# Every weight tile as three 256-column products, with one displacement between weights and moving tiles in SBUF

## The chip, the core and the metric

The kernel runs on one core of a Trainium2 chip. The metric is the device time of one execution in microseconds. The kernel before takes 1125.85 us, the median of three runs (1125.81 to 1126.93).

## What is computed

A trunk of two layers (DEPTH = 2) works on 256 positions of 1024 channels in float32. Each layer is a gated feed-forward block, a mixer, and a second feed-forward block, each behind an RMS norm and added to the residual; a last RMS norm ends it.

```python
for l in range(DEPTH):
    x = x + 0.5 * swiglu_ffn(rmsnorm(x, norm_ffn1[l]), ffn1_w_up[l], ffn1_w_down[l])
    x = x + hybrid_mixer(rmsnorm(x, norm_mix[l]), w_in[l], pool_w[l], pool_b[l], ...)
    x = x + 0.5 * swiglu_ffn(rmsnorm(x, norm_ffn2[l]), ffn2_w_up[l], ffn2_w_down[l])
return rmsnorm(x, final_norm)
...
def swiglu_ffn(h, w_up, w_down):
    a, b = jnp.split(h @ w_up, 2, axis=-1)
    return (jax.nn.silu(a) * b) @ w_down
```

The up weights are 1024 x 5632, the down weights 2816 x 1024. The mixer projects 1024 channels to 5120 (a pooling branch of 4 groups, a recurrent branch of 10 heads, a GELU branch, gate logits), sends the two branches through projections of their own, and ends with a 1024 x 1024 output projection (w_out).

## The kernel before, in words

**Weight tiles.** All weights come from DRAM as one stream of 128 x 128 tiles in the order in which they are used, 3152 of them, 8 to a transfer (`raw`). Each float32 value is split in two fp32r parts: ACT writes the high part (`wh`, a Copy at L219), DVE the low one (`wl`, a subtraction at L228). The moving tiles are split in the same way: high and low part of the 256 positions lie beside each other. A product of weights and activations is the sum wh·xh + wh·xl + wl·xh.

**Two forms of a tile.** `mm` (L309 to L320) makes three matmuls of 256 columns into one half of a PSUM bank (L316: wh·xh, L317: wh·xl, L318: wl·xh). `mm_wide` (L322 to L332) makes two: wl·xh, 256 columns, into the bank's first half (L329), and wh over both parts of x, 512 columns, into the whole bank (L330). After it the bank's second half holds wh·xl, which has to be added to the first.

```python
t.matmul(ps.t[:, 0, :], lhsT=wl(), rhs=x()[:, 0, :], start=start, stop=False, skip_group_check=True)
t.matmul(ps.t, lhsT=wh(), rhs=x(), start=False, stop=stop, skip_group_check=True)
```

**Which stage uses which.** The feed-forward blocks (`ffn`, L414) and the mixer's output projection (`out_mm`, L711) use the wide form; the rest of the mixer uses `mm`, and so does the very last output tile. Of the 3152 tiles 2218 are wide: four up products of 352 tiles with the moving tile XS, four down products of 176 (the last one 154) with GA and GB, two output projections of 64 with MU and MI. The other 934 are narrow: XS 640, ZHL 160, PHL 72, VHL 40, GA and GB 22.

**Evacuation.** In `evac` (L424) each up result of the wide form takes an ACT copy of the bank's second half and a DVE addition, twice per hidden tile, then one DVE multiplication with the norm's factor `rt` over 512 columns, SiLU on ACT, the gate's product on DVE and the split. In `new_x` (L393) the wide form takes an ACT copy into `sd` and a DVE addition beside the residual's update. Narrow pairs are evacuated by `scaled` (L384): one DVE multiplication of 512 columns straight from the bank, whose two halves hold two results.

**Order.** A planner (`Plan.schedule`, L123) orders DVE and ACT by due times that it reckons from costs, T_MM and T_MM_WIDE among them (L193, L194); PE and the transfers keep the program's order. The planner's costs are not measured by the program.

**Places in SBUF.** Pools are laid out one behind the other: the single tiles (XS among them), `raw`, `wh`/`wl`, a filler tile named `shift` (L846), then the large tiles by tag in the order in which they are first asked for. The tiles' sizes are multiples of 512 bytes except U, which has 10360 bytes. The built program has these first bytes of a partition:

| tile | first byte | modulo 512 | weights' place minus the tile's, modulo 512 |
|---|---|---|---|
| wh, wl (all 16) | 68864 and on | 256 | |
| XS | 24736 | 160 | +96 |
| VHL, ZHL, GA; GB | 134432; 156960 | 288 | -32 |
| MU | 189728 | 288 | -32 |
| PHL; MI | 210336; 218528 | 416 | -160 |
| acc; ones (the norm's moving tile and its weights) | 44736; 42112 | 192; 128 | -64 between these two |

A weight tile is 512 bytes of a partition, so within a chunk every tile has the same place modulo 512, and so has every moving tile of one name.

Of the kernel before, what the change touches and what calls it, by code (L numbers as in the profile page):

```python
# [8 lines left out]
F32 = mybir.dt.float32  # L9
F32R = mybir.dt.float32r  # L10
AF = mybir.ActivationFunctionType
ALU = mybir.AluOpType

D = 1024
S = 256
DEPTH = 2
KD = D // 128
FF = 2816
KF = FF // 128
# [4 lines left out]
NH = 10  # L24
CW = 4
# [11 lines left out]
HEAD = [[2, 2, 4], [4, 4], [4, 4], [4, 4]]  # L37
NRAW = 5
NSPL = 8
WARM = 7  # L40


# [147 lines left out]
    return 0.068 + 0.001042 * n + 0.06 * ptrs  # L190


T_MM = 0.327  # L193
T_MM_WIDE = 0.3245  # L194
KH = KF // 2


class Trunk:
# [120 lines left out]

        self.plan.add("PE", T_MM, fn, keys + list(r), [(ps, half)])  # L320

    def mm_wide(self, tag, ps, x, r, start, stop):  # L322

        wh, wl, keys = self.next_tile(tag)

        def fn():
            t = self.env.nc.tensor

            t.matmul(ps.t[:, 0, :], lhsT=wl(), rhs=x()[:, 0, :], start=start, stop=False, skip_group_check=True)  # L329
            t.matmul(ps.t, lhsT=wh(), rhs=x(), start=False, stop=stop, skip_group_check=True)  # L330

        self.plan.add("PE", T_MM_WIDE, fn, keys + list(r), [(ps, 0), (ps, 1)])  # L332


    def prep_x(self, m, gain, key):

# [41 lines left out]
    def x(self, m):  # L378
        return self.X.t[:, KD + m * S:KD + (m + 1) * S]
# [10 lines left out]
        self.mm(tag, ps, half, lambda: self.XS.t[:, k, 0, :], lambda: self.XS.t[:, k, 1, :],  # L390
                [(self.XS, (k, 0)), (self.XS, (k, 1))], k == 0, k == KD - 1)

    def new_x(self, m, ps, scale, gain, wide):  # L393
        X = self.X
        if wide:
            L = self.sd
            low = lambda: L.t
            self.act(low, lambda: ps.t[:, 1, :], AF.Copy, [(ps, 1)], [(L, 0)], S, scale=scale)
        self.stt(lambda: self.x(m), lambda: ps.t[:, 0, :], scale, lambda: self.x(m), ALU.mult, ALU.add,
                 [(ps, 0), (X, m)], [(X, m)], S)  # L400
        if wide:
            self.tt(lambda: self.x(m), lambda: self.x(m), low, ALU.add, [(X, m), (L, 0)], [(X, m)], S)
        if gain is not None:
            self.prep_x(m, self.par(gain + m), (self.prm, 0))
        self.prep_sq(m, gain is not None or m < KD - 1)
        if gain is None:
            if m == 0:
                self.XF = self.big("U", "XF", [128, KD, S], F32)
            XF = self.XF
            self.act(lambda: XF.t[:, m, :], lambda: self.x(m), AF.Copy, [(X, m), (self.prm, 0)], [(XF, m)], S,  # L410
                     scale=self.par(P_FIN + m))


    def ffn(self, l, wu, wd, gain, first):  # L414
        halves = (self.big("A", "GA", [128, KH, 2, S], F32R), self.big("B", "GB", [128, KH, 2, S], F32R))
        FT = self.big("V", "FT", [128, NH, S], F32)
        final = gain is None
        last = []

        def g(j):  # L420
            b = halves[j // KH]
            return b, (lambda: b.t[:, j % KH, :, :]), (b, (j, 0)), (b, (j, 1))

        def evac(j, ps):  # L424
            a, c = 2 * (j % 3), 6 + j % 3
            for h in range(2):
                t = lambda h=h: FT.t[:, a + h, :]
                self.act(t, lambda h=h: ps[h].t[:, 1, :], AF.Copy, [(ps[h], 1)], [(FT, a + h)], S)
                self.tt(t, lambda h=h: ps[h].t[:, 0, :], t, ALU.add, [(ps[h], 0), (FT, a + h)], [(FT, a + h)], S)
            both = lambda: FT.t[:, a:a + 2, :]  # L430
            tk = [(FT, a), (FT, a + 1)]
            self.tt(both, both, lambda: self.rt.t[:, None, :].to_broadcast([128, 2, S]), ALU.mult, tk + [(self.rt, 0)], tk,
                    2 * S)
            s = lambda: FT.t[:, c, :]
            last.append(self.act(s, lambda: FT.t[:, a, :], AF.Silu, [(FT, a)], [(FT, c)], S))
            self.tt(s, s, lambda: FT.t[:, a + 1, :], ALU.mult, [(FT, a + 1), (FT, c)], [(FT, c)], S)
            _, v, hi, lo = g(j)
            self.split(lambda: v()[:, 0, :], lambda: v()[:, 1, :], s, [(FT, c)], [hi], [lo], S)

        def up(ps, h, j, k):  # L440
            self.mm_wide((wu, l, k, h * KF + j), ps, lambda: self.XS.t[:, k, :, :],
                         [(self.XS, (k, 0)), (self.XS, (k, 1))], k == 0, k == KD - 1)

        ps = {}
        for h in range(2):
            for j in range(2):
                ps[j, h] = self.psum()
            for k in range(KD):
                for j in range(2):
                    up(ps[j, h], h, j, k)  # L450
                if h == (1 if first else 0) and k == (7 if first else 5):
                    self.norm_r(AF.Silu)
        for j in range(KF):
            if j >= 2:
                for h in range(2):
                    ps[j, h] = self.psum()
                    for k in range(KD):
                        up(ps[j, h], h, j, k)
            evac(j, (ps[j, 0], ps[j, 1]))
        self.preload(AF.Sqrt, last)  # L460
        for m in range(KD):
            pm = self.psum()
            wide = not (final and m == KD - 1)
            for k in range(KF):
                _, v, hi, lo = g(k)
                tag = (wd, l, k, m)
                if wide:
                    self.mm_wide(tag, pm, v, [hi, lo], k == 0, k == KF - 1)
                else:
                    self.mm(tag, pm, 0, lambda v=v: v()[:, 0, :], lambda v=v: v()[:, 1, :], [hi, lo], k == 0, k == KF - 1)  # L470
            self.new_x(m, pm, 0.5, gain, wide)


    def mixer(self, l, gain):
# [8 lines left out]
        g_at = 0  # L483
        u_at = KD * S
        s_at = u_at + PG * UW
        U = self.big("U", "U", [128, NH, CW - 1 + S], F32)
        V = self.big("V", "V", [128, NH, S], F32)
        TT = self.big("T", "TT", [128, NH, S], F32)
        PHL = self.big("P", "PHL", [128, 2 * PG, S], F32R)

        def G(m, n=1):
            return lambda: MB.t[:, g_at + m * S:g_at + (m + n) * S].rearrange("p (m t) -> p m t", t=S)
# [22 lines left out]
        ps = [self.psum(), self.psum()]  # L515
# [8 lines left out]
        for g in range(PG):  # L524
            sh = 1 << g
            lo = 2 * sh - 1
# [79 lines left out]


        R = self.big("U", "R", [128, NH, S], F32)
        I = self.big("I", "I", [128, NH, S], F32)

        def lru_gates(hs):
            for h in hs:
# [97 lines left out]

        def out_mm(ps, m, k):  # L711
            v, hi, lo = ms(k)
            self.mm_wide(("w_out", l, k, m), ps, v, [hi, lo], k == 0, k == KD - 1)

        ps = [self.psum(), self.psum()]
        for k in range(KD):
# [2 lines left out]
        for m in range(KD):  # L719
            if m >= 2:  # L720
                ps.append(self.psum())
                for k in range(KD):
                    out_mm(ps[m], m, k)
            self.new_x(m, ps[m], 1.0, gain, True)


    def softplus(self):
# [35 lines left out]
    def build(self):  # L763
# [1 line left out]
        self.head = [("L", 0), ("G", 0), ("L", 1), ("G", 1), ("L", 2), ("G", 2), ("L", 3), ("M", 0), ("L", 4), ("G", 3)]  # L765
        self.total = DEPTH * (2 * (2 * KF * KD + KD * KF) + 40 * KD + PG + 2 * NH + KD * PG + KD * NH + KD * KD)
        self.X = self.one("XG", [128, KD + KD * S])
        self.XS = self.one("XS", [128, KD, 2, S], F32R)
        self.prm = self.one("prm", [128, P_COLS])
        self.ones = self.one("ones", [128, 128])  # L770
        self.eps = self.one("eps", [128, 1])
# [66 lines left out]
def tile_trunk(ctx: ExitStack, tc: tile.TileContext, xt: bass.AP, par: bass.AP, wts: bass.AP, out: bass.AP):  # L838
# [4 lines left out]
    env.rawp = ctx.enter_context(tc.tile_pool(name="rawp", bufs=NRAW))  # L843
    env.splp = ctx.enter_context(tc.tile_pool(name="splp", bufs=NSPL))

    ctx.enter_context(tc.tile_pool(name="shift", bufs=1)).tile([128, 8], F32, name="shift")  # L846
    env.big = ctx.enter_context(tc.tile_pool(name="big", bufs=1))
    env.psp = ctx.enter_context(tc.tile_pool(name="psp", bufs=8, space=bass.MemoryType.PSUM))
    trunk.env = env
# [55 lines left out]
```

## Time and profile before

| | us |
|---|---|
| median of three runs | 1125.85 |
| the profiled execution | 1125.13 |
| its span, first to last instruction | 1123.4 |
| PE busy in it | 1109.6 (99%) |
| DVE busy | 885.2 (79%) |
| ACT busy | 691.1 (62%) |
| mean granted TensorE clock, share of full speed | 0.997 |

PE is the matmul stream, PEld the loading of weights into the array, which runs beside it. A matmul's record is longer than the distance to the next one's start, since matmuls are pipelined; the rate of the stream is read from starts, not from durations.

### The profile page before, as it was taken

How to read it: one execution, taken by the hardware profiler on the slowest of the kernel's cores; microseconds unless marked ns; L12 is line 12 of the kernel's file. 1: busy time of each engine (PE TensorE's matmuls, PEld its weight loads, DVE VectorE, ACT ScalarE, POOL GpSimd, SP SyncE). 2: the span in 40 equal slices, each digit the busy share in tenths (PEclk: the TensorE clock that was granted, in tenths of full speed). 3: DMA queues.
4: the chain of work that ended last, by engine and by line, in shares of the span. 5: the costliest groups of instructions: out<-in, count | busy, mean ns of one | idle time of the engine just before them, and what ended most of it. 6: DMA issues, size and time to landing. Idle time of an engine off the chain costs nothing.

```text
span 1123.4 us, 18938 instructions
## 1 busy us (share of the span) xinstructions
PE 1109.6 (99%) x7268; PEld 1016.8 (91%) x7268; DVE 885.2 (79%) x1384; ACT 691.1 (62%) x1133; POOL 0.2 (0%) x4
## 2 busy tenths in 40 slices
PE   8999999999999999999999999999999999999996
PEld 7888889999999888888888888899999998888886
DVE  7998766898988987776687777669989788777752
ACT  8766655559765765565565556555686666555641
POOL 0000000000000000000000000000000000000000
PEclk9999999999999999999999999999999999999998
DMA  8856666556656566666666666665476566666631
GB/s 287 271 180 205 188 188 189 185 170 191 193 182 188 188 191 191 192 192 189 188 188 188 189 189 192 195 182 185 142 229 184 173 205 187 189 188 189 188 111 38
DMA packets 59130, 210.03 MB, mean 187 GB/s; under 512 B 6560, under 2 KB 7456, under 8 KB 59040
## 3 DMA queue, kind: packets, MB, share of 16 engines
q1 hardware_dynamic: 59040, 208.82, 60.5%
q8 instruction: 57, 0.93, 0.3%
q14 instruction: 33, 0.27, 0.1%
HBM read 207.75 MB, written 1.05 MB: 186 GB/s over the span
## 4 chain that ended last, share of the span: by engine, by line
PE 98%; DMA 1%; DVE 0%; SPq 0%; ACT 0%; issue 0%; DVEq 0%; ACTq 0%
PE ps L330 45%; PE ps L329 23%; PE ps L316 10%; PE ps L317 10%; PE ps L318 10%; DMA XG<-in_x 1%; PE ps L360 0%; DVE XF L228 0%; DVE rt L370 0%; SPq L277 0%; SPq L791 0%; ACT XS L219 0%; PE ps L366 0%; DVE wl L228 0%; DVEq L900 0%
## 5 line engine op out<-in xcount | busy, mean ns | idle before, releaser
L219 ACT ACTIVATE wh<-raw 128x1024 fp32r<-128x1024 f32 (+2 forms) x399 | 418.3, 1050 | 365.3 <-PE ps L330 269.2
L228 DVE TENSOR_TENSOR wl<-raw,wh 128x1024 fp32r<-128x1024 f32 (+2 forms) x399 | 481.9, 1210 | 184.3 <-ACT wh L219 181.2
L330 PE MATMUL ps<-XS,wh 128*128 128x512 f32 x1408 | 488.7, 392 | 0.0
L329 PE MATMUL ps<-XS,wl 128*128 128x256 f32 x1408 | 394.7, 280 | 3.8 <-DVE wl L228 3.8
L330 PEld LDWEIGHTS ps<-XS,wh 128*128 128x128 f32 x1408 | 264.3, 188 | 58.2
L329 PEld LDWEIGHTS ps<-XS,wl 128*128 128x128 f32 x1408 | 264.3, 188 | 5.2 <-DVE wl L228 5.0
L316 PE MATMUL ps<-XS,wh 128*128 128x256 f32 x640 | 180.6, 282 | 0.0
L318 PE MATMUL ps<-XS,wl 128*128 128x256 f32 x640 | 180.2, 282 | 0.0
L317 PE MATMUL ps<-XS,wh 128*128 128x256 f32 x640 | 180.2, 282 | 0.0
L317 PEld LDWEIGHTS ps<-XS,wh 128*128 128x128 f32 x640 | 121.4, 190 | 0.1
L316 PEld LDWEIGHTS ps<-XS,wh 128*128 128x128 f32 x640 | 121.4, 190 | 0.1
L318 PEld LDWEIGHTS ps<-XS,wl 128*128 128x128 f32 x640 | 121.4, 190 | 0.0
L330 PE MATMUL ps<-GA,wh 128*128 128x512 f32 x341 | 119.6, 390 | 0.0
L330 PE MATMUL ps<-GB,wh 128*128 128x512 f32 x341 | 119.6, 390 | 0.0
L329 PE MATMUL ps<-GB,wl 128*128 128x256 f32 x341 | 96.2, 282 | 0.0
L329 PE MATMUL ps<-GA,wl 128*128 128x256 f32 x341 | 96.2, 282 | 0.0
L330 PEld LDWEIGHTS ps<-GA,wh 128*128 128x128 f32 x341 | 64.0, 188 | 13.4
L330 PEld LDWEIGHTS ps<-GB,wh 128*128 128x128 f32 x341 | 64.0, 188 | 13.4
L228 DVE TENSOR_TENSOR FT<-ps,FT 128x256 f32<-128x256 f32 x176 | 72.9, 416 | 1.8 <-ACT FT L219 1.7
L219 ACT ACTIVATE FT<-ps 128x256 f32<-128x256 f32 x176 | 64.3, 368 | 4.5 <-PE ps L330 4.1
L329 PEld LDWEIGHTS ps<-GB,wl 128*128 128x128 f32 x341 | 64.4, 189 | 0.0
L329 PEld LDWEIGHTS ps<-GA,wl 128*128 128x128 f32 x341 | 64.4, 189 | 0.0
(127 smaller groups left out, 1226.3 us busy)
## 6 DMA issues: line engine op xcount, KB each, us to landing
raw<-in_w SPq DMA_DIRECT2D x390, 512.0 KB, 4.2
raw<-in_w SPq DMA_DIRECT2D x7, 256.0 KB, 6.2
XG<-in_x SPq DMA_DIRECT2D x3, 256.0 KB, 6.0
out<-XF SPq DMA_DIRECT2D x3, 256.0 KB, 2.3
raw<-in_w SPq DMA_DIRECT2D x2, 128.0 KB, 3.1
out<-XF SPq DMA_DIRECT2D x2, 128.0 KB, 2.1
XG<-in_x SPq DMA_DIRECT2D x1, 132.0 KB, 2.6
XG<-in_x SPq DMA_DIRECT2D x1, 128.0 KB, 3.2
```

Source lines behind the costliest of these rows:

```text
L219: self.env.nc.scalar.activation(out=out(), in_=in_(), func=func, scale=scale if isinstance(scale, float) else scale(), **kw)
L228: return self.dve(t_dve(n), lambda v: v.tensor_tensor(out=out(), in0=a(), in1=b(), op=op), r, w)
L316: t.matmul(out, lhsT=wh(), rhs=xh(), start=start, stop=False)
L317: t.matmul(out, lhsT=wh(), rhs=xl(), start=False, stop=False)
L318: t.matmul(out, lhsT=wl(), rhs=xh(), start=False, stop=stop)
L329: t.matmul(ps.t[:, 0, :], lhsT=wl(), rhs=x()[:, 0, :], start=start, stop=False, skip_group_check=True)
L330: t.matmul(ps.t, lhsT=wh(), rhs=x(), start=False, stop=stop, skip_group_check=True)
```

## The change

All tiles take `mm`, three products of 256 columns into half a bank; `mm_wide` and its additions are gone, and the evacuation of the feed-forward blocks is `scaled`, one operation for a hidden tile's two results. The filler tile grows from 32 to 448 bytes (SHIFT = 112 values), XS moves behind it into a pool of its own, and the mixer's U is asked for after I, so that no tile behind it is displaced by its odd size. In the built program wh and wl begin at 52480 (256 modulo 512), and XS, VHL, ZHL, GA, GB, PHL, MI and MU all at places that are 192 modulo 512: the weights' place minus the moving tile's is +64 everywhere. The planner's cost of a tile is 0.341. The order of the weight stream and of its transfers stays.

```diff
-T_MM = 0.327
-T_MM_WIDE = 0.3245
+SHIFT = 112
+T_MM = 0.341
...
-    def mm_wide(self, tag, ps, x, r, start, stop):
...
-    def new_x(self, m, ps, scale, gain, wide):
+    def new_x(self, m, ps, scale, gain):
         X = self.X
-        if wide:
-            L = self.sd
-            low = lambda: L.t
-            self.act(low, lambda: ps.t[:, 1, :], AF.Copy, [(ps, 1)], [(L, 0)], S, scale=scale)
         self.stt(lambda: self.x(m), lambda: ps.t[:, 0, :], scale, lambda: self.x(m), ALU.mult, ALU.add,
                  [(ps, 0), (X, m)], [(X, m)], S)
-        if wide:
-            self.tt(lambda: self.x(m), lambda: self.x(m), low, ALU.add, [(X, m), (L, 0)], [(X, m)], S)
...
         def evac(j, ps):
             a, c = 2 * (j % 3), 6 + j % 3
-            for h in range(2):
-                t = lambda h=h: FT.t[:, a + h, :]
-                self.act(t, lambda h=h: ps[h].t[:, 1, :], AF.Copy, [(ps[h], 1)], [(FT, a + h)], S)
-                self.tt(t, lambda h=h: ps[h].t[:, 0, :], t, ALU.add, [(ps[h], 0), (FT, a + h)], [(FT, a + h)], S)
-            both = lambda: FT.t[:, a:a + 2, :]
-            tk = [(FT, a), (FT, a + 1)]
-            self.tt(both, both, lambda: self.rt.t[:, None, :].to_broadcast([128, 2, S]), ALU.mult, tk + [(self.rt, 0)], tk,
-                    2 * S)
+            self.scaled(ps, lambda: FT.t[:, a:a + 2, :], [(FT, a), (FT, a + 1)])
...
-        def up(ps, h, j, k):
-            self.mm_wide((wu, l, k, h * KF + j), ps, lambda: self.XS.t[:, k, :, :],
-                         [(self.XS, (k, 0)), (self.XS, (k, 1))], k == 0, k == KD - 1)
+        def up(h, j, k):
+            self.xmm((wu, l, k, h * KF + j), ps[j], h, k)
...
-        U = self.big("U", "U", [128, NH, CW - 1 + S], F32)
         V = self.big("V", "V", [128, NH, S], F32)
         TT = self.big("T", "TT", [128, NH, S], F32)
         PHL = self.big("P", "PHL", [128, 2 * PG, S], F32R)
+        I = self.big("I", "I", [128, NH, S], F32)
+        U = self.big("U", "U", [128, NH, CW - 1 + S], F32)
...
-            self.mm_wide(("w_out", l, k, m), ps, v, [hi, lo], k == 0, k == KD - 1)
+            self.mm(("w_out", l, k, m), ps, 0, lambda: v()[:, 0, :], lambda: v()[:, 1, :], [hi, lo], k == 0, k == KD - 1)
...
-        self.XS = self.one("XS", [128, KD, 2, S], F32R)
+        self.XS = Buf(self.plan, lambda: self.env.xsp.tile([128, KD, 2, S], F32R, name="XS"))
...
-    ctx.enter_context(tc.tile_pool(name="shift", bufs=1)).tile([128, 8], F32, name="shift")
+    ctx.enter_context(tc.tile_pool(name="shift", bufs=1)).tile([128, SHIFT], F32, name="shift")
+    env.xsp = ctx.enter_context(tc.tile_pool(name="xsp", bufs=1))
     env.big = ctx.enter_context(tc.tile_pool(name="big", bufs=1))
```

What stands in the two programs shows it at two places. On PE, in the first up product around the first norm's product (ps are banks, wh and wl the two parts of a chunk of weights, acc the squares' sum), before:

```order
L329 MATMUL ps_109<-XS_77,wl_100 128x256
L330 MATMUL ps_109<-XS_77,wh_99 128x512
L329 MATMUL ps_110<-XS_77,wl_100 128x256
L330 MATMUL ps_110<-XS_77,wh_99 128x512
L360 MATMUL ps_111<-acc_84,ones_79 128x256
L329 MATMUL ps_112<-XS_77,wl_103 128x256
L330 MATMUL ps_112<-XS_77,wh_102 128x512
```

and now:

```order
L316 MATMUL ps_111<-XS_80,wh_102 128x256
L317 MATMUL ps_111<-XS_80,wh_102 128x256
L318 MATMUL ps_111<-XS_80,wl_103 128x256
L348 MATMUL ps_112<-acc_87,ones_82 128x256
L316 MATMUL ps_113<-XS_80,wh_105 128x256
L317 MATMUL ps_113<-XS_80,wh_105 128x256
L318 MATMUL ps_113<-XS_80,wl_106 128x256
```

Two instructions with two weight loads became three with three, the columns stay 768, and the high part is now asked for first.

On DVE, late in the first up product, where the last hidden tiles are evacuated (FT holds their two halves, GB the hidden tile), before:

```order
L228 TENSOR_TENSOR FT_106<-ps_1237,FT_106 128x256
L228 TENSOR_TENSOR FT_106<-FT_106 128x256
L228 TENSOR_TENSOR wl_1455<-raw_1339,wh_1454 128x1024
L228 TENSOR_TENSOR FT_106<-ps_1264,FT_106 128x256
L228 TENSOR_TENSOR GB_105<-FT_106,GB_105 128x256
L228 TENSOR_TENSOR FT_106<-FT_106,rt_82 128x512
L228 TENSOR_TENSOR wl_1482<-raw_1366,wh_1481 128x1024
```

and now:

```order
L228 TENSOR_TENSOR GB_108<-FT_109,GB_108 128x256
L228 TENSOR_TENSOR wl_1640<-raw_1505,wh_1639 128x1024
L228 TENSOR_TENSOR FT_109<-ps_1121,rt_85 128x512
L228 TENSOR_TENSOR wl_1675<-raw_1536,wh_1674 128x1024
L228 TENSOR_TENSOR FT_109<-FT_109 128x256
```

The two additions from the banks are gone, and the multiplication with rt reads the bank itself.

## Rows read from the trace of the kernel before

**Rows 1.** The page: busy time and instructions, and the chain that ended last.

```profile
PE 1109.6 (99%) x7268; PEld 1016.8 (91%) x7268; DVE 885.2 (79%) x1384; ACT 691.1 (62%) x1133; POOL 0.2 (0%) x4
...
PE 98%; DMA 1%; DVE 0%; SPq 0%; ACT 0%; issue 0%; DVEq 0%; ACTq 0%
```

**Rows 2.** The waits of PE: total us, times, longest.

```profile
PE ps L329 <- DVE wl L228: 3.8, 4, 1.9
```

**Rows 3.** Timeline of PE, first and last of the stream: start us, us.

```profile
4.74 0.38 PE L329 MATMUL ps<-XS,wl 128*128 128x256 f32 x1 [0.34 <-DVE wl L228]
...
1113.14 0.59 PE L360 MATMUL ps<-acc,ones 128*128 128x256 f32 x2
```

**Rows 4.** Groups of PE, shapes apart: count, busy us, mean ns, idle before.

```profile
L330 PE MATMUL ps<-XS,wh 128*128 128x512 f32 x1408 | 488.7, 392 | 0.0
...
L330 PE MATMUL ps<-GA,wh 128*128 128x512 f32 x341 | 119.6, 390 | 0.0
L330 PE MATMUL ps<-GB,wh 128*128 128x512 f32 x341 | 119.6, 390 | 0.0
L329 PE MATMUL ps<-GB,wl 128*128 128x256 f32 x341 | 96.2, 282 | 0.0
...
L330 PE MATMUL ps<-MI,wh 128*128 128x512 f32 x64 | 22.8, 392 | 0.0
L330 PE MATMUL ps<-MU,wh 128*128 128x512 f32 x64 | 22.8, 390 | 0.0
...
L360 PE MATMUL ps<-acc,ones 128*128 128x256 f32 x14 | 4.2, 378 | 0.0
```

**Rows 5.** Timeline of PE in an up product, wide, XS: nine tiles apart.

```profile
400.36 0.39 PE L330 MATMUL ps<-XS,wh 128*128 128x512 f32 x1
...
403.48 0.39 PE L330 MATMUL ps<-XS,wh 128*128 128x512 f32 x1
```

**Rows 6.** Timeline of PE in a down product, wide, GB and GA: nine tiles apart.

```profile
520.31 0.39 PE L330 MATMUL ps<-GB,wh 128*128 128x512 f32 x1
...
523.43 0.39 PE L330 MATMUL ps<-GA,wh 128*128 128x512 f32 x1
```

**Rows 7.** Timeline of PE in the mixer's GELU projection, narrow, XS: 24 products apart.

```profile
300.05 0.28 PE L316 MATMUL ps<-XS,wh 128*128 128x256 f32 x1
...
302.93 0.28 PE L316 MATMUL ps<-XS,wh 128*128 128x256 f32 x1
```

**Rows 8.** Timeline of PE in the recurrent branch's projection, narrow, ZHL: 24 products apart.

```profile
335.12 0.28 PE L316 MATMUL ps<-ZHL,wh 128*128 128x256 f32 x1
...
337.92 0.28 PE L316 MATMUL ps<-ZHL,wh 128*128 128x256 f32 x1
```

**Rows 9.** Timeline of the weight loads at the first tile.

```profile
4.74 0.19 PEld L329 LDWEIGHTS ps<-XS,wl 128*128 128x128 f32 x1 [0.64 <-DVE wl L228]
4.85 0.19 PEld L330 LDWEIGHTS ps<-XS,wh 128*128 128x128 f32 x1
```

**Rows 10.** Stretches: the mixer up to w_out, its GELU and gate projections, an up product.

```profile
192.60:355.40 162.80, 162.80 (x1371) 162.73 (x1370) 143.20 (x214) 108.97 (x157) 0.00 (x0) 1.00 0.60 184
275.60:327.40 51.80, 51.80 (x434) 51.80 (x433) 48.36 (x68) 38.30 (x50) 0.00 (x0) 1.00 0.57 179
...
377.60:500.10 122.50, 122.50 (x708) 107.84 (x707) 98.92 (x160) 74.47 (x136) 0.00 (x0) 1.00 0.63 189
```

The columns of Rows 10 are the stretch, its length, then busy us and instructions of PE, PEld, DVE, ACT and POOL, the granted clock, the DMA engines' share and GB/s.

**Rows 11.** Groups of DVE and ACT that the change removes or rewrites.

```profile
L228 DVE TENSOR_TENSOR FT<-ps,FT 128x256 f32<-128x256 f32 x176 | 72.9, 416 | 1.8 <-ACT FT L219 1.7
L219 ACT ACTIVATE FT<-ps 128x256 f32<-128x256 f32 x176 | 64.3, 368 | 4.5 <-PE ps L330 4.1
L228 DVE TENSOR_TENSOR FT<-FT,rt 128x512 f32<-128x512 f32 x88 | 60.1, 684 | 0.1
...
L228 DVE TENSOR_TENSOR XG<-XG,sd 128x256 f32<-128x256 f32 x47 | 19.8, 421 | 0.6
...
L219 ACT ACTIVATE sd<-ps 128x256 f32<-128x256 f32 x47 | 17.8, 378 | 24.3 <-PE ps L330 23.0 <-DVE XG L233 1.1
```

More of the change, by code (lines that the diff above doesn't have):

```diff
@@ L320, in mm @@
         self.plan.add("PE", T_MM, fn, keys + list(r), [(ps, half)])
-    def mm_wide(self, tag, ps, x, r, start, stop):
[L324 to L332, printed above, removed]
     def prep_x(self, m, gain, key):
@@ L416, in ffn @@
         FT = self.big("V", "FT", [128, NH, S], F32)
-        final = gain is None
         last = []
@@ L438, in evac @@
             self.split(lambda: v()[:, 0, :], lambda: v()[:, 1, :], s, [(FT, c)], [hi], [lo], S)
-        def up(ps, h, j, k):
-            self.mm_wide((wu, l, k, h * KF + j), ps, lambda: self.XS.t[:, k, :, :],
-                         [(self.XS, (k, 0)), (self.XS, (k, 1))], k == 0, k == KD - 1)
-        ps = {}
+        def up(h, j, k):
+            self.xmm((wu, l, k, h * KF + j), ps[j], h, k)
+        ps = [self.psum(), self.psum()]
         for h in range(2):
-            for j in range(2):
-                ps[j, h] = self.psum()
             for k in range(KD):
                 for j in range(2):
-                    up(ps[j, h], h, j, k)
+                    up(h, j, k)
                 if h == (1 if first else 0) and k == (7 if first else 5):
@@ L454, in ffn @@
             if j >= 2:
+                ps.append(self.psum())
                 for h in range(2):
-                    ps[j, h] = self.psum()
                     for k in range(KD):
-                        up(ps[j, h], h, j, k)
-            evac(j, (ps[j, 0], ps[j, 1]))
+                        up(h, j, k)
+            evac(j, ps[j])
         self.preload(AF.Sqrt, last)
@@ L462, in ffn @@
             pm = self.psum()
-            wide = not (final and m == KD - 1)
             for k in range(KF):
                 _, v, hi, lo = g(k)
[L466 to L471, printed above, removed]
+                self.mm((wd, l, k, m), pm, 0, lambda v=v: v()[:, 0, :], lambda v=v: v()[:, 1, :], [hi, lo], k == 0,
+                        k == KF - 1)
+            self.new_x(m, pm, 0.5, gain)
     def mixer(self, l, gain):
@@ L608, in mixer @@
         R = self.big("U", "R", [128, NH, S], F32)
-        I = self.big("I", "I", [128, NH, S], F32)
         def lru_gates(hs):
@@ L723, in mixer @@
                     out_mm(ps[m], m, k)
-            self.new_x(m, ps[m], 1.0, gain, True)
+            self.new_x(m, ps[m], 1.0, gain)
     def softplus(self):
```

## The prediction

> **What bounds the kernel now.** I read the page first: PE is busy for 99% of the span and the chain that ended last lies on PE for 98% [rows 1]. Then the waits: PE stands still for a DVE-made low part four times, 3.8 us in all, in the head, and for nothing else of size [rows 2]. So the time is that of the matmul stream, and the question is what a weight tile costs in it. The stream begins at 4.74 us and the last norm's product follows it at 1113.14 us [rows 3]: 1108.4 us. From this go the 3.8 us of waits and six norm products; two records of such a product take 0.59 us and one 0.378 us, so the second begins 0.21 us after the first, and a product is some 0.42 us, six of them 2.5 us [rows 3, 4]. That leaves 1102.1 us for 3152 tiles, **0.350 us a tile**; what is not tiles in the execution of 1125.13 us is 23.0 us.
>
> The two forms differ. Nine wide tiles take 3.12 us, 0.347 us each, with XS as with GB and GA [rows 5, 6]. The 2218 wide tiles [rows 4] are then 769 us, and the 934 narrow ones share the other 333 us, 0.357 us each. That agrees with the mixer up to w_out, 162.8 us with one norm product for 456 narrow tiles, 0.356 us each [rows 10]. But a narrow tile has no single price: 24 products take 2.88 us with XS, 120.0 ns each, and 2.80 us with ZHL, 116.7 ns each [rows 7, 8], which is 0.360 and 0.350 us a tile.
>
> How much of that is the array's own? A record of 512 columns is 390 ns where one of 256 is 282 ns [rows 4]: 256 more columns are 108 ns. Weight loads that wait for no matmul start 0.11 us apart [rows 9], so the load isn't slower than that. Three products at 108 ns are 0.324 us. Every tile thus pays 23 to 36 ns above its columns, while nothing in the profile is waited for. The same instruction, with the same engines beside it, pays 9 ns a product with ZHL and 12 ns with XS; what differs is which bytes the weight load and the moving stream read at the same time. The places of the table above fit a look at that: XS stands at +96 and ZHL at -32.
>
> **What the table says about +64.** The three displacements before, +96, -32 and -160, are all 96 modulo 128. The new one isn't: it is 64 modulo 128, and no fp32r stream of this trace runs there. The one stream of that kind is the norm's product, acc against ones, at -64: its two records stand 0.21 us apart [rows 3, 4], two times 106 ns, with a weight load beside it, so without the extra that every tile pays. It works in plain float32 and takes two records for one product (14 for seven), so it shows that a load can go beside a matmul for nothing, not that +64 does it.
>
> **The change part by part.**
>
> *The products.* 2218 tiles go from two products to three and from 0.347 us to the narrow price; 934 stay narrow and change their displacement alone. The price at +64 is the one unknown, and it is bounded by rows: 108 ns a product from below (columns alone), 120.0 ns from above (the dearest narrow stream seen, and the row whose displacement is nearest, +96). The planner's 0.341 is no price: for the tiles that it put at 0.327 the rows show 0.350 and 0.360. I take **114 ns**, the middle, because the row nearest in place (120) and the row nearest in kind, a displacement of 64 modulo 128 (106), point to opposite ends. That is 0.342 us a tile, 3152 x 0.342 = 1078.0 us, and with the 23.0 us of the rest 1101.0 us.
>
> *Weight loads.* 2218 more of them. A wide tile hides its second load under 512 columns; now each load has 256 columns to hide under, 107 to 110 ns against 108 ns, so none has slack. This is in the 120 ns and 116.7 ns rows already, which are streams of that kind.
>
> *Evacuation.* Gone are 176 + 47 additions on DVE, 92.7 us, and as many copies on ACT, 82.1 us; the 88 multiplications of 684 ns stay and read the bank [rows 11]. All of it lies beside PE, so it is worth nothing in the sum. The multiplication now waits for both halves of the bank and for rt; behind it on DVE stand splits of weights whose buffers hold 64 tiles, some 22 us of PE's work, so PE doesn't see that wait. A hidden tile holds one bank where it held two, which only frees banks.
>
> *DVE in the mixer.* There the change removes nothing. DVE is busy for 143.2 of 162.8 us, and for 48.4 of the 51.8 us of the GELU and gate projections, 144 tiles [rows 10]. At 0.342 us these take 49.2 us: DVE is at 98% and still fits; where it slips, the 22 us of split weights cover it. I count nothing.
>
> *Head and tail.* The high part is now asked for first, so at each of the four waits [rows 2] two products could start before the low part is there, 0.23 us: at most 0.9 us in all, not counted. The last tile was narrow before, and the tail behind 1113.14 us stays. Transfers keep their order and their queue; they run at 184 to 189 GB/s [rows 10] and follow PE.
>
> Sum: **1101 us**, 24 us less. The profiled execution lies 0.7 us under the median of the runs, so the same sum against the median is 1101.7 us. A measurement of this kernel can tell about 0.2%, 2.3 us, from no change.
>
> **The rivals.**
>
> *Placement is nothing, and the third product costs (slower).* If the extra belongs to each pair of load and matmul, whatever the bytes, all tiles take the average narrow price, 0.357 us: 23.0 + 3152 x 0.357 = 1148 us; with every tile at the 120.0 ns of XS, 1158 us. It decides from 0.350 us a tile upwards. For it: the nearest displacement, +96, is the dearest, and narrow tiles are dearer than wide ones in every stage seen. Against it: the same form has two prices within one mixer [rows 7, 8].
>
> The Trainium skill speaks for this rival: TensorE: Matmul & The Clock Gate, in "Step-by-step: what each phase is for", says that the array has two independent read ports into SBUF, so that loading the next weights takes no bandwidth from the running matmul. By the formula under "Back-to-back issue gap" of the same page, 2.5 ns above N/2.4, a narrow tile would be 327.5 ns and a wide one 325.0 ns; by it the change costs 2218 x 2.5 ns = 5.5 us, an estimate from that page, 1131 us. The trace disagrees with the formula, with 347 and 350 to 360 ns [rows 5 to 8].
>
> *As at -32 (no change).* If +64 behaves like ZHL's displacement, a tile is 0.350 us, just the average of now: 23.0 + 1103.2 = 1126.2 us. For it: the two wide streams differ little although their displacements do.
>
> *No extra at all (much faster).* If +64 is free as the norm's product is, a tile is 0.324 us and the sum 1044 us; then the GELU projections would take 46.7 us where DVE has 48.4 us of work, and DVE would give back up to 2 x 1.7 us, 1048 us. Against it: each load then has no slack at all.
>
> **How the numbers follow.** A smaller extra, 0.331 to 0.347 us a tile, 1066 to 1117 us: 0.55, likeliest because the change leaves the class of displacement that all streams share. Almost no extra, 1044 to 1066 us: 0.07. As at -32, 1117 to 1133 us: 0.10, of which 0.07 lie within 2.3 us of before and 0.015 on each side. The narrow price of now, 1139 to 1158 us: 0.28. So faster 0.55 + 0.07 + 0.015, some 0.63, same 0.07, slower 0.28 + 0.015, some 0.30. The range leaves out the lowest case and the dearer part of the slow one, some 0.2 together: 1068 to 1150 us; the likeliest case alone has 1066 to 1117 us.
>
> **What would show it right or wrong.** Right: PE still at 99%, no new wait of PE outside the head, and starts of narrow products equally far apart with XS, ZHL, GA and MU, near 114 ns, in every stage; DVE near 793 us and ACT near 609 us busy. Wrong in the first term: starts of 117 to 120 ns with a time of 1126 us or more. Wrong in the covers: PE waiting for wl or ZHL in the GELU projections. Different spacings in stages of one displacement would say that the displacement doesn't set the price by itself.

## The result and the profile after

The changed kernel takes 1136.24 us (median of 4, 1135.81 to 1137.48) where the kernel before, beside it, takes 1125.91 us: ratio 1.0092, 95% interval 1.008 to 1.0104. It is 0.9% **slower**. The forecast was faster; the time lies inside the range that was given.

The page of the changed kernel, with the lines that answer to [rows 1]:

```profile
PE 1122.9 (99%) x9486; PEld 1120.4 (99%) x9486; DVE 822.7 (73%) x1161; ACT 625.5 (55%) x909; POOL 0.2 (0%) x4
...
PE 98%; DMA 0%; DVE 0%; SPq 0%; ACT 0%; issue 0%; DVEq 0%; ACTq 0%
```

PE is still the bound, with 2218 more products. On the same page DVE now idles 32.5 us in all for PE before the multiplication that evacuates a hidden tile; PE doesn't wait for it. The waits of PE for weights (engine and line, releaser: us in total, times, longest); its two other waits, 1.0 us ahead of the stream and 0.6 us in the tail, are as long as before:

```profile
PE ps L316 <- ACT wh L219: 0.8, 2, 0.6
PE ps L318 <- DVE wl L228: 0.4, 2, 0.2
```

Against [rows 2] the waits in the head got shorter, 3.8 us for low parts to 0.4 us for low and 0.8 us for high ones, and no new one stands in the middle. So the time went into the spacing of the products. PE's timeline of the changed kernel (start us, us), in three stages: the GELU projection with XS, the recurrent branch with ZHL, a down product with GA. In each pair the second row begins 24 products after the first:

```profile
299.95 0.28 PE L316 MATMUL ps<-XS,wh 128*128 128x256 f32 x1
...
302.78 0.28 PE L316 MATMUL ps<-XS,wh 128*128 128x256 f32 x1
...
334.93 0.28 PE L316 MATMUL ps<-ZHL,wh 128*128 128x256 f32 x1
...
337.76 0.28 PE L316 MATMUL ps<-ZHL,wh 128*128 128x256 f32 x1
...
519.80 0.28 PE L316 MATMUL ps<-GA,wh 128*128 128x256 f32 x1
...
522.63 0.28 PE L316 MATMUL ps<-GA,wh 128*128 128x256 f32 x1
```

All three are 2.83 us: 117.9 ns a product whatever the moving tile, where [rows 7, 8] had 120.0 ns for one and 116.7 ns for the other. Over whole stages the starts average 117.8 ns, **353.3 ns a tile**. The prediction's own formula with this price, 23.0 + 3152 x 0.3533, gives 1136.6 us, 0.4 us above the measured median.

But one stage differs. The same view in the head, up to the first norm's product (L348):

```profile
15.69 0.28 PE L316 MATMUL ps<-XS,wh 128*128 128x256 f32 x1
...
18.41 0.28 PE L316 MATMUL ps<-XS,wh 128*128 128x256 f32 x1
...
18.78 0.70 PE L348 MATMUL ps<-acc,ones 128*128 128x256 f32 x2
...
```

From 15.69 to 18.41 us are 24 products in 2.72 us: **113.3 ns** each, 340.0 ns a tile, with the same instruction, the same XS and the same displacement of +64 bytes. Behind the norm's product the stream settles at 117.8 ns and never comes back. From here on the spacing of 113.3 ns is called the cheap one and that of 117.8 ns the dear one. The stretches of 9.0 to 18.7 us and of the GELU and gate projections (length, then busy us and count of PE, PEld, DVE, ACT and POOL, the granted clock, DMA share, GB/s):

```profile
9.00:18.70 9.70, 9.50 (x82) 9.30 (x81) 9.25 (x23) 9.11 (x19) 0.00 (x0) 1.00 1.04 410
277.00:327.90 50.90, 50.90 (x435) 50.90 (x434) 48.76 (x67) 38.22 (x51) 0.00 (x0) 1.00 0.56 178
```

So the cheap spacing shows where DVE (95% busy), ACT (94%) and the transfers (410 GB/s) are at their densest, the dear one where they have more room, at the same granted clock of 1.00. It isn't the load of the other engines.

That left two questions: what the form and the place each cost, and what the norm's product does to the stream.

### The profile page after: what moved, and what is told of

It is laid out like the page before. It is cut to its first block, busy times and chain, and to the rows that moved or that the text cites. A ratio compares the mean times of both kernels' runs of the same rounds, so it can differ in the third digit from the quotient of the medians.

```text
span 1134.0 us, 22803 instructions
## 1 busy us (share of the span) xinstructions
PE 1122.9 (99%) x9486; PEld 1120.4 (99%) x9486; DVE 822.7 (73%) x1161; ACT 625.5 (55%) x909; POOL 0.2 (0%) x4
## 4 chain that ended last, share of the span: by engine, by line
PE 98%; DMA 0%; DVE 0%; SPq 0%; ACT 0%; issue 0%; DVEq 0%; ACTq 0%
PE ps L318 33%; PE ps L317 33%; PE ps L316 33%; DMA raw<-in_w 0%; PE ps L348 0%; DVE XF L228 0%; DVE rt L358 0%; SPq L758 0%; SPq L277 0%; PE ps L354 0%; DVE wl L228 0%; ACT wh L219 0%; DVEq L868 0%; ACT sd L219 0%; DVE XG L233 0%
## 5 line engine op out<-in xcount | busy, mean ns | idle before, releaser
L316 PE MATMUL ps<-XS,wh 128*128 128x256 f32 x2048 | 577.2, 282 | 0.8 <-ACT wh L219 0.8
L317 PE MATMUL ps<-XS,wh 128*128 128x256 f32 x2048 | 575.7, 281 | 0.0
L317 PEld LDWEIGHTS ps<-XS,wh 128*128 128x128 f32 x2048 | 391.9, 191 | 0.2
L316 PEld LDWEIGHTS ps<-XS,wh 128*128 128x128 f32 x2048 | 386.1, 189 | 1.7 <-ACT wh L219 1.5
L316 PE MATMUL ps<-GA,wh 128*128 128x256 f32 x352 | 98.9, 281 | 0.0
L318 PE MATMUL ps<-GB,wl 128*128 128x256 f32 x352 | 98.9, 281 | 0.0
L316 PE MATMUL ps<-GB,wh 128*128 128x256 f32 x352 | 98.9, 281 | 0.0
L318 PE MATMUL ps<-GA,wl 128*128 128x256 f32 x352 | 98.9, 281 | 0.0
L317 PE MATMUL ps<-GA,wh 128*128 128x256 f32 x352 | 98.9, 281 | 0.0
L317 PE MATMUL ps<-GB,wh 128*128 128x256 f32 x352 | 98.9, 281 | 0.0
L228 DVE TENSOR_TENSOR FT<-ps,rt 128x512 f32<-128x512 f32 x88 | 60.5, 691 | 33.1 <-PE ps L318 32.5
L317 PEld LDWEIGHTS ps<-GB,wh 128*128 128x128 f32 x352 | 67.2, 191 | 0.0
L317 PEld LDWEIGHTS ps<-GA,wh 128*128 128x128 f32 x352 | 67.2, 191 | 0.0
L316 PEld LDWEIGHTS ps<-GB,wh 128*128 128x128 f32 x352 | 66.5, 189 | 0.0
L316 PEld LDWEIGHTS ps<-GA,wh 128*128 128x128 f32 x352 | 66.5, 189 | 0.0
L219 ACT ACTIVATE GB<-FT 128x256 fp32r<-128x256 f32 x44 | 18.3, 416 | 52.8 <-DVE FT L228 52.8
```

Of the source, the lines that this page charges most:

```text
L219: self.env.nc.scalar.activation(out=out(), in_=in_(), func=func, scale=scale if isinstance(scale, float) else scale(), **kw)
L228: return self.dve(t_dve(n), lambda v: v.tensor_tensor(out=out(), in0=a(), in1=b(), op=op), r, w)
L316: t.matmul(out, lhsT=wh(), rhs=xh(), start=start, stop=False)
L317: t.matmul(out, lhsT=wh(), rhs=xl(), start=False, stop=False)
L318: t.matmul(out, lhsT=wl(), rhs=xh(), start=False, stop=stop)
```

## The experiments

All prices below are means of the distances between starts on PE's timeline over whole stages, three products to a tile; rows are shown for a few.

### The form without the place, and the place without the form

`a_narrow_old_places` is the changed kernel with the tiles laid as before:

```diff
-SHIFT = 112
+SHIFT = 8
...
-        self.XS = Buf(self.plan, lambda: self.env.xsp.tile([128, KD, 2, S], F32R, name="XS"))
+        self.XS = self.one("XS", [128, KD, 2, S], F32R)
```

with U and I back in their old order as well.

> All tiles as three products, at the places of the kernel before (+96, -32, -160). Two theories of where the 10 us come from. Form: three loads cost what they cost wherever the bytes lie; then every stream is near the changed kernel's 117.8 ns a product, 353.3 ns a tile, and the time is near 1136 us. Place: the streams keep the prices that narrow tiles had at these places before, 350 ns a tile with GA, GB and MU (-32), 352 to 360 with XS (+96) and MI (-160); with some 2048 tiles of XS at 357 that is about 23 + 731 + 386 = 1140 to 1150 us, and stages differ from each other.

Measured: 1142.76 us (1141.17 to 1145.02) beside 1125.06 us, ratio 1.0155 (1.0134 to 1.0175). Its timeline of PE, the GELU projection with XS (+96) and a down product with GB (-32), 24 products apart:

```profile
299.75 0.28 PE L316 MATMUL ps<-XS,wh 128*128 128x256 f32 x1
...
302.63 0.28 PE L316 MATMUL ps<-XS,wh 128*128 128x256 f32 x1
...
519.83 0.28 PE L316 MATMUL ps<-GB,wh 128*128 128x256 f32 x1
...
522.63 0.28 PE L316 MATMUL ps<-GB,wh 128*128 128x256 f32 x1
```

120.0 and 116.7 ns: GB, wide before, takes ZHL's price of [rows 8] once it is narrow at the same displacement, and stages differ from each other as the theory of the place had it. The third product costs 17.7 us at the old places; moving the bytes then gives 6.5 us back (1142.76 to 1136.24). But XS at +96 has no single price either: the four up products behind a norm run at 360.0, 356.0, 360.0 and 356.0 ns a tile, with the same instructions at the same places, and at each of the five later norms XS has one spacing ahead of the norm's product and another behind it (359.9 and 356.0 ns at the second).

`b_wide_new_places` keeps the new places and restores the two forms, `mm_wide` and its evacuation, word for word:

```diff
+    def mm_wide(self, tag, ps, x, r, start, stop):
...
+            t.matmul(ps.t[:, 0, :], lhsT=wl(), rhs=x()[:, 0, :], start=start, stop=False, skip_group_check=True)
+            t.matmul(ps.t, lhsT=wh(), rhs=x(), start=False, stop=stop, skip_group_check=True)
```

> The two forms of the kernel before, all tiles at the new places (+64). If the form costs the 10 us and the place nothing: wide tiles stay at 347 ns, narrow ones fall a little to 353 ns, 1123 us. If the place pays and the third product takes it back: wide tiles fall clearly below 347 ns, towards 330, and the time is 1080 to 1110 us. If the new place is worse for wide tiles: above 347 ns, over 1130 us.

Measured: 1138.03 us (1137.91 to 1138.49), ratio 1.0111 (1.0096 to 1.0126). Nine wide tiles in a down product of this kernel, to be laid beside [rows 6]:

```profile
519.89 0.40 PE L330 MATMUL ps<-GB,wh 128*128 128x512 f32 x1
...
523.07 0.40 PE L330 MATMUL ps<-GA,wh 128*128 128x512 f32 x1
```

3.18 us for nine, 0.353 us a tile, against 3.12 us before. This kernel has the instructions of the kernel before, and only the bytes lie elsewhere: it is 1.1% slower. So the place matters. As these streams ran, +64 is worse than -32 and +96 for wide tiles (0.353 against 0.347 us); for narrow ones, in the dear spacing, it lies between -32 (350.0 ns) and +96 (352 to 360.0 ns). In b's trace the wide tiles show no cheaper spacing, in the head neither; whether something else behind the norm would bring one was not tried with wide tiles. The Trainium skill (TensorE: Matmul & The Clock Gate, "Step-by-step: what each phase is for") has the next weights load through a read port of its own, so that they take no SBUF read bandwidth from the running matmul. If a place could act through that bandwidth alone, b would have kept 1125 us; it took 1138.03 us, and by what path the place acts no run here shows.

### What stands between two tiles

`c_pause_after_norm` puts, behind each norm product but the last, a small fp32r product of 128 columns that must wait for an ACT copy of the norm's result:

```diff
+            NR = self.big("P", "NR", [128, 2 * PG, S], F32R)
+            pz = self.psum()
+            self.act(lambda: NR.t[:, 0, 0:128], lambda: ps.t[:, 0, 0:128], AF.Copy, [(ps, 0)], [(NR, 0)], 128)
...
+                lambda: self.env.nc.tensor.matmul(pz.t[:, 0, 0:128], lhsT=NR.t[:, 0, 0:128], rhs=NR.t[:, 0, 0:128], start=True,
...
```

Its product is read by nobody. The tile NR takes the buffer of PHL, which is asked for later.

> The changed kernel, and behind each norm product but the last PE waits for an ACT copy of its result and makes one small product of it, which is used nowhere: a pause of half a microsecond to a microsecond, six times. Lock theory: at +64 the stream has two steady spacings, 113.4 ns as ahead of the first norm product and 117.8 ns as behind it, and a pause lets it fall back into the first; then 340 ns a tile for nearly all of 3152 tiles, 1095 to 1103 us. Rival: the spacing depends on something that changes for good about 19 us into the kernel (the other engines' load, the stage); then 117.8 ns stays and the time is 1136 us and some 4 us for the pauses, 1140 us.

Measured: 1099.75 us (1099.55 to 1107.16), ratio 0.9786 (0.9754 to 0.9819), with 340.0 ns a tile in every stage of the profiled execution (1099.57 us). Its timeline of PE at the first norm (in brackets the idle time before a row and what ended it):

```profile
19.46 0.59 PE L348 MATMUL ps<-acc,ones 128*128 128x256 f32 x2
20.43 0.33 PE L362 MATMUL ps<-NR 128*128 128x128 f32 x1 [0.37 <-ACT NR L219]
...
20.99 0.28 PE L316 MATMUL ps<-XS,wh 128*128 128x256 f32 x1
...
21.67 0.28 PE L316 MATMUL ps<-XS,wh 128*128 128x256 f32 x1
```

Six products in 0.68 us, 113.3 ns. Added work and added waits make the kernel 36 us faster than the change. One execution of the four took 1107.16 us, some 7.5 us more; 13.3 ns on the 508 to 528 tiles between two norms come to 6.8 to 7.0 us, so one such stretch in the dear spacing would give most of it, but this execution has no trace. That left open whether the wait or the product did it, and whether it was the norm's float32 that had thrown the stream.

`d_norm_in_two_parts` computes the norm by two fp32r products, of the high and the low part of acc, with a copy of ones as the weights; `e_norm_parts_at_64` is the same with that copy 64 bytes further:

```diff
+                t.matmul(ps.t[:, 0, :], lhsT=NR.t[:, 2, 0:128], rhs=NR.t[:, 0, :], start=True, stop=False)
+                t.matmul(ps.t[:, 0, :], lhsT=NR.t[:, 2, 0:128], rhs=NR.t[:, 1, :], start=False, stop=True)
```

```diff
-                t.matmul(ps.t[:, 0, :], lhsT=NR.t[:, 2, 0:128], rhs=NR.t[:, 0, :], start=True, stop=False)
+                t.matmul(ps.t[:, 0, :], lhsT=NR.t[:, 2, 16:144], rhs=NR.t[:, 0, :], start=True, stop=False)
...
```

> The changed kernel with the norm product (all but the last) as two fp32r products of a split sum instead of one float32 product, without a pause meant. If the float32 product throws the stream out of the cheap spacing: 113.4 ns in every stage, 340 ns a tile, 1093 to 1100 us. If any interruption does it: 117.8 ns behind the first norm, 1133 to 1136 us. If the other engines' load does it: 117.8 ns from about 19 us on, whatever stands at the norm, 1133 to 1136 us.

Measured: 1129.6 us (1129.16 to 1136.25, 7 executions), ratio 1.0055 (1.0033 to 1.0077). Its timeline of PE at the second norm:

```profile
192.56 0.28 PE L316 MATMUL ps<-XS,wh 128*128 128x256 f32 x1
...
193.24 0.28 PE L316 MATMUL ps<-XS,wh 128*128 128x256 f32 x1
...
193.58 0.28 PE L358 MATMUL ps<-NR 128*128 128x256 f32 x1
193.70 0.28 PE L359 MATMUL ps<-NR 128*128 128x256 f32 x1
193.81 0.28 PE L316 MATMUL ps<-XS,wh 128*128 128x256 f32 x1
...
194.17 0.28 PE L316 MATMUL ps<-XS,wh 128*128 128x256 f32 x1
```

Six products in 0.68 us ahead of it (113.3 ns), three in 0.36 us behind it, and 353.3 ns a tile from there to the end. Two fp32r products at a displacement of 0, with no idle time and no float32, have thrown the stream. At the first norm, where the second part was waited for (0.43 us between the two), the stream stayed cheap.

> As the run with the norm in two fp32r parts, but its weights of ones now stand 64 bytes past the parts' place too, so that the norm's two products are like any others. Theory now: at +64 the stream has two steady spacings, 113.3 and 117.8 ns; it keeps the one it is in, a product at another displacement without a pause throws it into the dearer one, and a start from rest ends in the cheaper one. Then nothing throws it: 340.0 ns a tile in every stage, no pause, 1091 to 1096 us. Rival: any change of tile or weights that isn't a weight tile throws it, or the mixer's stages do; then 353.3 ns from the second norm on, 1129 us as in the run with the parts at another displacement.

Measured: 1094.52 us, ratio 0.9727 (0.9706 to 0.9748), 340.0 ns a tile in every stage behind the first norm; with the parts at +64 too the stream runs through the norm as if it were another tile. Its timeline of PE at the second norm:

```profile
193.18 0.28 PE L358 MATMUL ps<-NR 128*128 128x256 f32 x1
193.29 0.28 PE L359 MATMUL ps<-NR 128*128 128x256 f32 x1
193.41 0.28 PE L316 MATMUL ps<-XS,wh 128*128 128x256 f32 x1
```

Of its four executions one took 1136.02 us, at a granted clock of 0.998 where the others had 0.997, and is not in the ratio; 3152 tiles at 13.3 ns are 42 us, so a stream that starts dear and meets nothing that changes it would give that time, but this execution has no trace.

`g_small_product_no_pause` is c with the small product's tile copied from ones, long before, so that nothing waits:

```diff
-            self.act(lambda: NR.t[:, 0, 0:128], lambda: ps.t[:, 0, 0:128], AF.Copy, [(ps, 0)], [(NR, 0)], 128)
+            self.act(lambda: NR.t[:, 0, 0:128], lambda: self.ones.t, AF.Copy, [(self.ones, 0)], [(NR, 0)], 128)
```

> The control of the run with the pause: the same small product of 128 columns behind each norm product, but of a tile that has long been ready, so that PE waits for nothing. If the pause is what brings the cheap spacing back: 353.3 ns a tile behind the first norm product, 1136 to 1138 us. If the small product does it: 340 ns, 1095 us.

Measured: 1094.88 us (one execution), 340.0 ns a tile throughout. If the pause were needed, it would have been 1136 to 1138 us; the idea that PE has to stand still **fell**. Timed as `g_small_product_timed`:

> The run with the small product of a ready tile behind each norm product again, timed: the one look gave 1094.9 us, 340 ns a tile throughout. If the spacing is set at each restart behind a norm, in the same way every time: all runs at 1094 to 1096 us. If it is a matter of luck at the start of an execution: some runs at 1136 us, as one of the four of the kernel with the norm in parts at +64.

1095.88 us (1094.7 to 1096.45, 5 executions) beside 1125.65 us, ratio 0.9735 (0.9721 to 0.975). It is faster than the kernel before and than the change. In its profile the stream came to the first norm already in the dear spacing; its timeline of PE there:

```profile
18.82 0.28 PE L316 MATMUL ps<-XS,wh 128*128 128x256 f32 x1
...
19.53 0.28 PE L316 MATMUL ps<-XS,wh 128*128 128x256 f32 x1
...
19.88 0.59 PE L348 MATMUL ps<-acc,ones 128*128 128x256 f32 x2
20.12 0.41 PE L362 MATMUL ps<-NR 128*128 128x128 f32 x1
...
20.77 0.28 PE L316 MATMUL ps<-XS,wh 128*128 128x256 f32 x1
...
21.11 0.28 PE L316 MATMUL ps<-XS,wh 128*128 128x256 f32 x1
```

Six products in 0.71 us (118 ns) ahead of it, three in 0.34 us (113.3 ns) behind it, and no idle time between. The small product doesn't only keep a cheap stream, it makes a dear one cheap.

`i_small_product_layer2_only` has it behind the norms of the second layer alone:

```diff
+            self.norms > 3 and self.plan.add(
```

> The small product behind the three norm products of the second layer alone. Theory: the stream keeps a spacing until something between two weight tiles shifts its start. Then 353.3 ns a tile from the first norm to the fourth, some 1540 tiles, and 340.0 ns behind it: 1094.9 + 1540 x 0.0133 = 1115 us, with the change of price at the fourth norm, near 565 us, without any pause. Rival: the small product only keeps a cheap spacing that it finds, and doesn't bring it back; then 353.3 ns from the first norm to the end, 1136 us.

Measured: 1117.07 us (one execution), 353.3 ns a tile from the first norm to the fourth and 340.0 ns behind it. At the fourth norm on PE's timeline:

```profile
566.81 0.28 PE L316 MATMUL ps<-GB,wh 128*128 128x256 f32 x1
...
569.63 0.28 PE L316 MATMUL ps<-XS,wh 128*128 128x256 f32 x1
...
571.76 0.59 PE L348 MATMUL ps<-acc,ones 128*128 128x256 f32 x2
572.00 0.41 PE L363 MATMUL ps<-NR 128*128 128x128 f32 x1
...
572.65 0.28 PE L316 MATMUL ps<-XS,wh 128*128 128x256 f32 x1
...
573.67 0.28 PE L316 MATMUL ps<-XS,wh 128*128 128x256 f32 x1
```

24 products in 2.82 us ahead of it, nine in 1.02 us behind: the switch lies at the first norm that has the added product behind it.

`j_product_of_256_columns` lets the added product have 256 columns instead of 128 (the tile's second half is copied from ones too):

```diff
-                lambda: self.env.nc.tensor.matmul(pz.t[:, 0, 0:128], lhsT=NR.t[:, 0, 0:128], rhs=NR.t[:, 0, 0:128], start=True,
+                lambda: self.env.nc.tensor.matmul(pz.t[:, 0, :], lhsT=NR.t[:, 0, 0:128], rhs=NR.t[:, 0, :], start=True,
```

> The product of a ready tile behind each norm product has 256 columns, not 128. If the moment of the restart decides: 256 columns take as long as a weight's product and shift nothing, so the dear spacing may stay, 353.3 ns, 1136 us; if any fp32r product between the float32 product and the weight tiles is enough: 340 ns, 1096 us.

Measured: 1136.9 us (one execution). At its first norm:

```profile
18.58 0.28 PE L316 MATMUL ps<-XS,wh 128*128 128x256 f32 x1
...
19.26 0.59 PE L348 MATMUL ps<-acc,ones 128*128 128x256 f32 x2
19.50 0.47 PE L363 MATMUL ps<-NR 128*128 128x256 f32 x1
19.81 0.28 PE L316 MATMUL ps<-XS,wh 128*128 128x256 f32 x1
...
21.93 0.28 PE L316 MATMUL ps<-XS,wh 128*128 128x256 f32 x1
```

Ahead of the norm six products take 0.68 us, 18.58 to 19.26 us, which is the cheap spacing; behind it 18 products take 2.12 us, 117.8 ns, and 353.3 ns a tile stays to the end. A product of the same kind at the same spot, only longer, neither keeps a cheap stream nor makes a dear one cheap. So "any fp32r product behind the norm" isn't the rule either; of the two lengths tried, one leads to the cheap spacing and the other to the dear one. That they act through the moment at which the tiles start again is argued, not shown.

### Other displacements

Two kernels, each c with another filler, put XS and the other tiles elsewhere:

```diff
-SHIFT = 112
+SHIFT = 120
...
+    ctx.enter_context(tc.tile_pool(name="shift2", bufs=1)).tile([128, 8], F32, name="shift2")
```

```diff
-SHIFT = 112
+SHIFT = 96
...
+    ctx.enter_context(tc.tile_pool(name="shift2", bufs=1)).tile([128, 48], F32, name="shift2")
```

> The kernel with the pauses, with two fillers: weights minus moving tile is +32 with XS and 0 with every other moving tile. If the displacement sets which spacings there are, XS and the others show two prices that differ from 340.0 and 353.3 ns, each constant over its stages unless it has two states as well; a price under 340 would be a better place. If only the pauses matter: 340 ns everywhere, 1100 us.

Measured: 1152.04 us. Its timeline of PE, 24 products of a down product at a displacement of 0:

```profile
149.79 0.28 PE L316 MATMUL ps<-GB,wh 128*128 128x256 f32 x1
...
152.67 0.28 PE L316 MATMUL ps<-GA,wh 128*128 128x256 f32 x1
```

> The same with +128 for XS and -64 for the other moving tiles, which is the displacement of the float32 norm product, whose records stood 0.21 us apart. If that product showed a place without extra: near 324 to 330 ns a tile with GA, GB, ZHL, MU and MI. If it showed a property of float32: a price between 340 and 360 ns there. XS: unknown, 340 to 360 ns.

Measured: 1147.57 us. The same stretch at -64:

```profile
149.93 0.28 PE L316 MATMUL ps<-GB,wh 128*128 128x256 f32 x1
...
152.76 0.28 PE L316 MATMUL ps<-GA,wh 128*128 128x256 f32 x1
```

2.88 and 2.83 us: 120.0 and 117.9 ns. With a's places the price of a three-product tile is (means over stages; behind a small product, which delays one tile, the mean of a stage is up to 0.4 ns higher):

| weights' place minus moving tile's, bytes modulo 512 | ns a tile | kernel |
|---|---|---|
| -160 | 355.0 to 359.9 | a_narrow_old_places |
| -64 | 353.3 | h_xs_at_128_others_at_minus_64 |
| -32 | 350.0, with VHL up to 353.6 | a_narrow_old_places |
| 0 | 360.0, in short stages from 358 | h_xs_at_32_others_at_0 |
| +32 | 355.0 to 355.4 | h_xs_at_32_others_at_0 |
| +64 | 340.0 or 353.3 | g and e, the change |
| +96 | 352.1, 356.0 or 360.0 | a_narrow_old_places |
| +128 | 355.6 to 356.4 | h_xs_at_128_others_at_minus_64 |

Both h kernels have c's small product and wait, and neither shows 340.0 anywhere in these stages: the cheap spacing was seen at +64 alone. Only multiples of 32 bytes were tried, and the two h kernels ran once each. The weight tiles stand at 256 modulo 512 in all of these kernels, so the table can't tell the displacement from the moving tile's own place; d and e alone move weights, those of the norm.

### Theory

At +64 the stream of three-product tiles has two steady spacings, 340.0 and 353.3 ns a tile, and keeps the one it is in until something else stands between two tiles. In the changed kernel the norm's product is that something, and each time it is followed by the dear one. Five runs bear on it from different sides: d switches to the dear one at its second norm without float32, e passes the same norm with nothing moved but its weights and stays cheap, g switches back without a pause, i switches back where the product is added and not before, j doesn't switch back when the product is longer. The head alone can end either way: dear in the profile of g_small_product_timed, cheap in that of the change. Several spacings at one displacement aren't special to +64 either: XS at +96 changes its own at norms (a).

The weight loads carry a mark of the two spacings. From 780 to 900 us the changed kernel (first two rows) and g_small_product_timed (last row) show, as PEld's groups (count, busy us, mean ns, idle before):

```profile
L317 PEld LDWEIGHTS ps<-XS,wh 128*128 128x128 f32 x244 | 46.8, 192 | 0.0
L316 PEld LDWEIGHTS ps<-XS,wh 128*128 128x128 f32 x244 | 45.8, 188 | 0.0
...
L317 PEld LDWEIGHTS ps<-XS,wh 128*128 128x128 f32 x168 | 31.5, 188 | 0.0
```

In the dear spacing one load of the three of each tile has a record of 192 ns and the two others 188 ns; in the cheap one all three have 188 ns. It is the same load in every tile from one norm to the next, but not always the same one: in the change it is L316 from the first norm to the second and L317 behind that, in d and j L316 at every stretch. So the dear stream repeats one pattern tile after tile, and the pattern too changes at a norm. Why there are two spacings, and what the load and the moving stream meet in, no record shows; that it is the moment of the restart is the reading that fits all of these, not a thing seen.

## Why the prediction was wrong

- **The term that failed** is the price at +64: "I take 114 ns, the middle, because the row nearest in place (120) and the row nearest in kind, a displacement of 64 modulo 128 (106), point to opposite ends." It measured 117.8 ns in all but the head; together with a time of 1136 us that is the prediction's own sign for "wrong in the first term". The 3.8 ns, over three products of 3152 tiles, come to 36 us, and the miss is 35 us, 1101 to 1136. The number itself exists, 113.3 ns, in the head and in c, e and g; what failed is the assumption behind it that a displacement has one price. The prediction named the sign for this, different spacings in stages of one displacement, and it came: the head against everything behind it.
- **The assumption could be read from the kernel before.** [rows 7] has XS at 0.360 us a tile. The same XS, narrow and at the same +96, earlier in that mixer:

```profile
209.73 0.28 PE L316 MATMUL ps<-XS,wh 128*128 128x256 f32 x1
...
213.29 0.28 PE L316 MATMUL ps<-XS,wh 128*128 128x256 f32 x1
```

These are 30 products in 3.56 us, 0.356 us a tile, and 0.356 us is the mean of all 132 tiles behind that norm. The prediction saw that a narrow tile has no single price and gave the whole difference to the displacement; one displacement already had two.
- **The class modulo 128** was no ground. 0 and +128 cost 360.0 and 356 ns, -64 and +64 cost 353.3 and 340.0 or 353.3, -32 and +96 cost 350.0 and 352 to 360.0. The norm's product at -64 was read as running without the extra [rows 3, 4], which takes its 0.21 us a record for two passes of 256 columns, and no row shows that. fp32r tiles at -64 pay 353.3 ns, so the place isn't free for them.
- **Which rival came true.** None in its words: at 353.3 ns a tile the time fell between "as at -32", which ended at 1133 us, and the narrow price of now, which began at 1139 us. The sign is that of "placement is nothing", and so is most of the size of the form's price: at unchanged places the third product costs 17.7 us (a), where that rival gave 22 us. But placement is not nothing: it cost 13 us with wide tiles (b), gave 6.5 us back with narrow ones (a against the change), and with another product behind the norm the same places are worth 40 us more (the change against g).
- **The formula of the Trainium skill** (TensorE: Matmul & The Clock Gate, "Back-to-back issue gap") gave 327.5 ns for a narrow tile. That section gives the formula for the isolated gap, and says that it under-counts at small N in a stream where each matmul has its weight load. The direction agrees with the runs at N = 256: the best stream here has 340.0 ns, and the eight displacements pay 13 to 33 ns more than the formula.
- **What held.** PE stayed the bound at 99%; no wait arose in the projections, where DVE was busy for 48.76 of 50.90 us; evacuation, DMA order and tail were worth nothing that shows. PE's waits for weights in the head fell by 2.6 us, where the prediction allowed at most 0.9 us and counted none. With the measured price the prediction's sum gives 1136.6 us, and with 0.340 it gives 1094.7 us, within 1.2 us of g's and e's medians. The 23.0 us of the rest was right to about a microsecond.
- **A smaller miss**, off the path: DVE fell from 885.2 to 822.7 us, not to 793, and ACT from 691.1 to 625.5, not to 609. The removed instructions' durations were subtracted whole, 92.7 and 82.1 us; the page's busy time fell by 62.5 and 65.6 us, as durations that overlap a neighbour's count once in it.
- **The range** held because its upper end took in the price of now. The chance of slower, 0.30, was too low: the only narrow rows were streams of 116.7 and 120.0 ns, 0.350 and 0.360 us a tile, and both are dearer than the 0.347 us of the 2218 wide tiles that were to become narrow. That the time came out inside the range says nothing for the mechanism.

## What to carry to other kernels

Where PE is the bound and nothing is waited for, measure the distance between product starts stage by stage: a few ns of it, over thousands of products, are the whole difference between 1095 and 1136 us, while the busy share of PE reads 99% either way. A spacing that changes within one displacement and one form is a sign that what stood between the stages matters, so look at the few foreign products in the stream before giving up on a layout. Here one product of 128 columns behind each norm makes the change worth 2.65% instead of -0.9%.

## What the runs showed that was not expected

- The same instructions on the same engines, their bytes moved, cost 1125 or 1138 us (b).
- In the dear spacing at +64 one weight load of each tile's three has a record 4 ns longer than the others, and which one it is changes at a norm (the change).
- A stream with no wait in it can run at 113.3 or 117.8 ns a product for hundreds of us, and a product of 128 columns without any idle time moves it from one to the other (g, i), while one of 256 columns does not (j).
- d's seven executions lie near 1129.5 and 1136.2 us. The difference, 6.7 us, is 13.3 ns times the some 500 tiles between the first norm and the second, so it fits a stream that already turned dear at the first norm; those executions were not profiled.
